# A hybrid SSM and attention layer on one core: the output product's weight sums made in DRAM during the attention, its operand sums made in DRAM and rounded in the middle of products, and the last residual tiles loaded into room of their own

## The chip, the cores and the metric

The kernel runs on one core of a Trainium2 chip. The metric is the device time of one execution in microseconds (us). A run executes the kernel and gives one time; a second record, the profiled execution, gives the span from the first to the last instruction and the trace of every engine and DMA.

The engines go by these names: PE (TensorE, matmuls), ACT (ScalarE), DVE (VectorE), POOL (GpSimd) and SP (SyncE, which only issues DMAs). ACT and POOL issue DMAs too. Each engine works its instructions in program order.

## What is computed

One encoder layer on a sequence of 512 rows of width 2048, all in float32: a state space scan on 4 groups (branch A, y) and an attention of 16 heads (branch B, o), merged by gates. Cut from the reference:

```
    h = rmsnorm(x, norm_w)
    u = h @ w_in
...
    y_fwd = ssd_scan(xs, dtf, a_f, bm, cm)
...
    y = y.reshape(b, s, D_SSM) * jax.nn.silu(z_ssm)
...
    o = bidir_attention(qn, qr, kn, kr, v) * jax.nn.silu(z_attn)

    merged = jax.nn.sigmoid(g_ssm) * (y @ w_proj_ssm) + jax.nn.sigmoid(g_attn) * (o @ w_proj_attn)
    return x + merged @ w_out
...
    return rmsnorm(x, final_norm_w)
```

The change touches `merged @ w_out`, the residual add and the last normalisation. Rows come in four tiles `t` of 128, columns in four blocks `b` of 512.

## The kernel before

**Arithmetic.** A float32 product is made of three matmuls on rounded parts: each operand x is split into a high part (a cast on ACT) and a low part (x minus high, on DVE), and PE does high x high, high x low and low x high (lines 605 to 607). `w_split` splits a weight chunk of 128 x 1024 this way (lines 433 and 434) into `wh` and `wl`, three buffers each. ACT and DVE do this for every chunk in program order, so whatever stands ahead of a chunk's split on ACT or DVE holds PE up once three chunks are used up.

**Stages.** Input projection, state space scan, attention, and then three products of 512 x 2048 x 2048, named by their weights `wps` (y), `wpa` (o) and `wo` (merged, the output product). Each is one level of Strassen: `pair(cp)` computes one half of the output columns by seven products P1 to P7, each with four weight chunks m = 0..3 and 48 matmuls. The order is P1, P5, P6, P2, P3, P7, P4, except for the first pair of `wo` (`early`): P1, P2, P5, P6, P3, P7, P4. The activation operands are x11, x12, x22 and sums S1 to S4. The weight operands are blocks of w and sums: T1 = w00 + w01, T2 = T1 + w11 (`t2`), T3 = w11 + w01, and T4 = T2 + w10 (`t4`). `X` and `Y` are four chunk buffers each; `wraw` has three.

**Where the sums are made before.** For `wps` and `wpa`, T1 and T3 are made in DRAM ahead of time: `t_jobs` yields a list of DMAs on POOL, a copy DRAM to DRAM of 512 KB and, two copies later, an accumulate onto it; `in_background(n)` issues the next n. The 32 of `wps` run in the scan, the 32 of `wpa` in the attention, four per head behind a small POOL multiply (`pace`) that waits for the head's softmax sums. For `wo` they are made in SBUF: `w_more` (line 532) lets POOL issue an accumulating DMA of w01 onto an `X` or `Y` chunk after its plain use.

The activation operands of `wo` are made from the results of `wpa`: `done_pa` turns each block on PE (`turn`), and ACT moves it out. Blocks of x11, x21 and S3 go to DRAM (`m_d`). S4 and x22 stand raw in SBUF (`m_raw`, placed by `m_room`), S2 raw in two `xraw` tiles; POOL's accumulating DMAs add the later blocks there (lines 1474 and 1482). `Merged.split` rounds a whole operand on ACT and DVE (lines 433, 434; 436 for S2, which has its sign turned): S2 after P2, S4 and x22 after P5, S3 after P6, by the table of hooks in `Strassen("wo", ...)`.

**The end.** A finished block of the output gets its residual: for t < 2 or b < 2 by an accumulating DMA of x on POOL (line 1649), else by a DVE add from a `gate` tile that POOL loads late (lines 1625, 1645). ACT squares each block with a running sum (line 1639, `scr`). `final_weights` loads the final gains broadcast (`fw`); `weigh` multiplies the blocks of t >= 2 by them on POOL (line 1636). `finish(t)` computes the row scale r and scales and stores the four blocks of a row tile: t = 0 and 1 one product after P3 of the second pair, t = 2 and 3 from the last product (`last_o`). All stores go out on SP.

Of the kernel before, what the change touches and what calls it, by code (L numbers as in the profile page):

```python
# [18 lines left out]
P = 128  # L19
# [53 lines left out]
def build(tc, a):  # L73
# [48 lines left out]
    m_d = {w: scratch(f"m_{w}", 2048) for w in ("x11", "x21", "S3")}  # L122
# [3 lines left out]
    t_d = {(w, cp, n): scratch(f"{n}_{w}{cp}", 4096) for w in ("wps", "wpa") for cp in range(2) for n in ("T1", "T3")}  # L126
# [273 lines left out]

    def za_gen(i):
        p_ = mm("za")
        yield from gemm_steps(p_, win(T_ZA + i), h_h, h_l)
        g_ = st("za")
        act.activation(g_, p_, AF.Silu)
        put(za_d[i], g_)

# [60 lines left out]
    class Merged:  # L468
# [9 lines left out]
        def load(self, which, src, tiles):  # L478
            self.raws[which] = tiles
            for q, t in enumerate(tiles):  # L480
                tc.keep_in_program_order(pool.dma_start(t, src[:, q * 1024:(q + 1) * 1024]))
# [22 lines left out]
    def t_jobs(w):  # L504

        jobs = []
        for cp in range(2):
            for name, kh, cb in (("T1", 0, 0), ("T3", 1, 1)):
                for m in range(4) if (w, cp, name) in t_d else ():
# [79 lines left out]
    def product(name, op, chunk, extra=None, pre=None):  # L589
# [3 lines left out]
        for m in range(4):  # L593
# [4 lines left out]
            if pre and m == 2:  # L598
# [31 lines left out]
    class Strassen:  # L630
# [65 lines left out]
        def pair(self, cp, headed=False, early=False):  # L696
# [44 lines left out]
            def t3(m, raw):  # L741
                w_more(raw, w, cp, 0, 1, m)
# [3 lines left out]
            p5 = evict((yield from product("P5", self.op("S1"), c5, t2)), "p5", self.kept("C22", cp))  # L746
            self.hook(cp, "P5")
            A = yield from product("P6", self.op("S2"), lambda m: X[m])
# [8 lines left out]
            B = yield from product("P3", self.op("S4"), lambda m: Y[m], None if made3 else t3,  # L757
# [421 lines left out]

    compressed(0, 6, rq_d, V_QN, cq_h, cq_l)  # L1180
# [6 lines left out]
    fill.run(36)  # L1187

# [24 lines left out]
    fill.run(36)  # L1213
    dve.tensor_scalar(ang2, ang, math.pi / 2, None, ALU.add)
# [5 lines left out]
    fill.run(48)  # L1220

# [113 lines left out]
    fill.until(("qk", 0))  # L1335
    fill.run(24)

    heads = {}
    in_background(len(background))
    background.extend(t_jobs("wpa"))  # L1340
    pace = few(1)

    def scores(hd, t):
# [16 lines left out]
        if background and t == 1:  # L1360
            pool.tensor_mul(pace, sm_, sm_)
            in_background(4)
# [90 lines left out]
    def done_pa(t, b, o):  # L1453
# [3 lines left out]
        def turn():  # L1457
# [13 lines left out]
            elif t < 2:  # L1471
                o_ = st("turned")
                act.activation(o_, tp, AF.Copy, scale=-1.0)
                pool.dma_start(m_ops.raw("S4", q, u), o_, accum_op=ALU.add)
                m_ops.into(w, o_, sl.start, SEQ)
            else:
                s1, raw = (m_ops.raw(n, q, u) for n in ("S1", "x22"))
                dve.tensor_sub(s1, s1, tp)
                act.activation(raw, tp, AF.Copy, scale=-1.0)
                m_ops.into("S1", s1, sl.start, SEQ)  # L1480
                for n in ("S2", "S4"):
                    pool.dma_start(m_ops.raw(n, q, u), raw, accum_op=ALU.add)
# [3 lines left out]
    m_ops = Merged()  # L1486

# [3 lines left out]
    def m_room():  # L1491
# [280 lines left out]
```

## Time and profile before

| what | value |
|---|---|
| three runs | 2051.38, 2042.46, 2047.32 us; median 2047.32 |
| the profiled execution | 2045.46 us, its span 2043.7 us |
| mean granted PE clock | 0.987 |
| busy: PE, DVE, ACT, POOL | 95%, 75%, 49%, 18% of the span |
| DMA moved | 393.25 MB, mean 192 GB/s |
| the output product on PE | 1842.93 to about 2028.5 us of the span |

How to read the rows: times are us from the start of the span. A row of an engine's timeline has start, duration, engine, source line, operation, output and inputs by the program's names, shape and count; in square brackets is the idle time of the engine before it and what ended that. A DMA row has the issuing queue, the KB of each and the median us from issue to landing. A row of waits has total, number and longest. Rows of the windows view have the stretch, its length, then busy time (and number of instructions) of PE, PE's weight load, DVE, ACT and POOL, the granted clock, the DMA share and GB/s.

### The profile page before, as it was taken

What the parts mean: (1) busy time and instruction counts of PE and PEld (TensorE: products, weight loads), DVE (VectorE), ACT (ScalarE), POOL (GpSimd) and SP (SyncE); (2) the same over time, 40 slices, a digit from 0 to 9 for tenths busy, and PEclk for the clock granted to TensorE, in tenths of its full rate; (3) what the DMA queues carried; (4) which work ended last, traced back from release to release, by engine and by line L of the source; (5) the groups of instructions that cost most, each with busy time, mean ns of one, the idle gap of its engine ahead of it and who ended that gap; (6) DMA issues with size and microseconds to landing.
All of it is one profiled execution on the core that took longest, in us unless ns stands there. A gap on an engine that the chain in (4) does not pass through costs nothing.

```text
span 2043.7 us, 24735 instructions
## 1 busy us (share of the span) xinstructions
PE 1945.2 (95%) x8978; PEld 1602.9 (78%) x8978; DVE 1532.7 (75%) x2016; ACT 1000.6 (49%) x1392; POOL 363.4 (18%) x405
## 2 busy tenths in 40 slices
PE   6999999999999999999999999999999999998796
PEld 5878888888878778787788788888877788886675
DVE  7976676676759889799795767667677898786675
ACT  6444445444544656546555344444455355444453
POOL 0001001001032252342430101110011110213113
PEclk9999999999999999999999999999999999999998
DMA  5568658647456747687574957873487886978746
GB/s 195 164 181 206 164 126 205 170 124 201 130 174 180 236 145 206 207 242 206 172 200 139 256 159 178 224 191 99 99 254 256 275 301 211 308 220 218 208 84 184
DMA packets 169898, 393.25 MB, mean 192 GB/s; under 512 B 16752, under 2 KB 61936, under 8 KB 169584
## 3 DMA queue, kind: packets, MB, share of 16 engines
q1 hardware_dynamic: 102384, 229.94, 34.4%
q0 software_dynamic: 36448, 119.03, 26.6%
q10 hardware_dynamic: 30944, 42.71, 5.8%
q8 instruction: 70, 1.15, 0.2%
q14 instruction: 52, 0.43, 0.1%
HBM read 334.47 MB, written 100.14 MB: 213 GB/s over the span
## 4 chain that ended last, share of the span: by engine, by line
PE 65%; DVE 13%; DMA 9%; issue 7%; ACT 3%; POOL 1%; SPq 0%; ACTq 0%; DVEq 0%; POOLq 0%
PE P L606 11%; PE P L607 11%; PE P L605 11%; PE za L168 2%; PE xbc L168 2%; PE za L169 2%; PE xbc L169 2%; PE za L170 2%; PE xbc L170 2%; DVE sum L1092 2%; DVE wl L434 2%; DVE wl L164 1%; DMA stack<-qr 1%; DMA wraw<-wps 1%; PE pb L1369 1%
## 5 line engine op out<-in xcount | busy, mean ns | idle before, releaser
L434 DVE TENSOR_TENSOR wl<-X,wh 128x1024 fp32r<-128x1024 f32 x180 | 219.4, 1223 | 100.9 <-ACT wh L433 100.8
L433 ACT CAST wh<-X 128x1024 fp32r<-128x1024 f32 x180 | 188.9, 1053 | 203.2 <-PE P L607 162.1
L164 DVE TENSOR_TENSOR wl<-wraw,wh 128x1024 fp32r<-128x1024 f32 (+2 forms) x148 | 176.4, 1192 | 82.4 <-ACT wh L163 80.2
L163 ACT CAST wh<-wraw 128x1024 fp32r<-128x1024 f32 (+2 forms) x150 | 145.0, 969 | 129.4 <-PE xbc L169 38.6
L434 DVE TENSOR_TENSOR wl<-Y,wh 128x1024 fp32r<-128x1024 f32 x96 | 117.1, 1223 | 79.1 <-ACT wh L433 79.1
L433 ACT CAST wh<-Y 128x1024 fp32r<-128x1024 f32 x96 | 100.9, 1053 | 137.0 <-PE P L607 104.3
L168 PE MATMUL xbc<-h_h,wh 128*128 128x512 f32 x384 | 152.7, 398 | 0.0
L170 PE MATMUL xbc<-h_h,wl 128*128 128x512 f32 x384 | 150.6, 392 | 0.0
L169 PE MATMUL xbc<-h_l,wh 128*128 128x512 f32 x384 | 150.4, 392 | 0.0
L606 PE MATMUL P<-wl,h_h 128*128 128x512 f32 x384 | 149.5, 389 | 0.0
L607 PE MATMUL P<-wh,h_l 128*128 128x512 f32 x384 | 149.4, 389 | 0.0
L605 PE MATMUL P<-wh,h_h 128*128 128x512 f32 x384 | 149.4, 389 | 0.0
L606 PE MATMUL P<-wl,S 128*128 128x512 f32 x288 | 112.5, 391 | 0.8 <-DVE wl L434 0.7
L607 PE MATMUL P<-wh,S 128*128 128x512 f32 x288 | 112.1, 389 | 0.0
L605 PE MATMUL P<-wh,S 128*128 128x512 f32 x288 | 112.1, 389 | 0.0
L168 PE MATMUL za<-h_h,wh 128*128 128x512 f32 x256 | 101.1, 395 | 0.0
L170 PE MATMUL za<-h_h,wl 128*128 128x512 f32 x256 | 99.9, 390 | 0.0
L169 PE MATMUL za<-h_l,wh 128*128 128x512 f32 x256 | 99.6, 389 | 0.0
L433 ACT CAST wh<-wraw 128x1024 fp32r<-128x1024 f32 x56 | 58.9, 1052 | 81.9 <-PE P L607 55.9
L434 DVE TENSOR_TENSOR wl<-wraw,wh 128x1024 fp32r<-128x1024 f32 x56 | 68.4, 1223 | 39.6 <-ACT wh L433 39.6
L1092 DVE TENSOR_TENSOR_SCAN sum<-da,scn 128x512 f32<-128x512 f32 x64 | 86.3, 1361 | 0.0
L1356 ACT ACTIVATE pr<-s,nm 128x512 f32<-128x512 f32 x64 | 44.2, 690 | 84.0 <-DVE nm L1354 83.2
(727 smaller groups left out, 5264.0 us busy)
## 6 DMA issues: line engine op xcount, KB each, us to landing
wraw<-wi SPq DMA_DIRECT2D x102, 512.0 KB, 4.0
T_wps<-wps POOLq DMA_DIRECT2D x32, 512.0 KB, 6.3
da<-da_d SPq DMA_DIRECT2D x64, 256.0 KB, 4.4
T_wpa<-wpa POOLq DMA_DIRECT2D x32, 512.0 KB, 9.2
wraw<-wps SPq DMA_DIRECT2D x24, 512.0 KB, 5.8
xbc_d<-xbc ACTq DMA_DIRECT2D x24, 256.0 KB, 3.3
wraw<-wun SPq DMA_DIRECT2D x16, 384.0 KB, 3.1
wraw<-wo SPq DMA_DIRECT2D x12, 512.0 KB, 4.1
```

The source lines that it names most:

```text
L163: act.copy(h, raw)
L164: (dve if ahead[0] else pool).tensor_sub(l, raw, h.bitcast(F32))
L168: pe.matmul(out, wh, xh, start=start, stop=False)
L169: pe.matmul(out, wh, xl, start=False, stop=False)
L170: pe.matmul(out, wl, xh, start=False, stop=stop)
L433: i = act.copy(hi_, raw)
L434: dve.tensor_sub(lo_, raw, hi_.bitcast(F32))
L605: pe.matmul(bs[i], xh, wh, start=(j == 0), stop=False)
L606: pe.matmul(bs[i], xh, wl, start=False, stop=False)
L607: pe.matmul(bs[i], xl, wh, start=False, stop=(j == 7))
L1092: dve.tensor_tensor_scan(sums[dd], flat(da), mask, 0.0, ALU.add, ALU.mult)
L1356: act.activation(pr, s, AF.Exp, bias=nm, scale=SCALE, accum_out=sm_)
```

## The change

The order of PE's instructions stays the same. The diff, cut to its core:

```
-    m_d = {w: scratch(f"m_{w}", 2048) for w in ("x11", "x21", "S3")}
+    m_d = {w: scratch(f"m_{w}", 2048) for w in ("x11", "x21", "S2", "S3", "S4")}
...
-    t_d = {(w, cp, n): scratch(f"{n}_{w}{cp}", 4096) for w in ("wps", "wpa") for cp in range(2) for n in ("T1", "T3")}
+    t_d = {(w, cp, n): scratch(f"{n}_{w}{cp}", 4096) for w in ("wps", "wpa", "wo") for cp in range(2) for n in ("T1", "T3")}
...
+    paced = [None]
+    pace = few(1)
+
+    def at_pace(t, n):
+        if background:
+            pool.tensor_mul(pace, t[:, 0:1], t[:, 0:1])
+            in_background(n)
...
             def t3(m, raw):
-                w_more(raw, w, cp, 0, 1, m)
+                if not made3:
+                    w_more(raw, w, cp, 0, 1, m)
                 if early:
                     t4_alone(m, raw)
...
+    in_background(len(background))
+    background.extend(t_jobs("wpa"))
+    background.extend(t_jobs("wo"))
     compressed(0, 6, rq_d, V_QN, cq_h, cq_l)
...
+    at_pace(paced[0], 3)
...
-        if background and t == 1:
-            pool.tensor_mul(pace, sm_, sm_)
-            in_background(4)
+        if t == 1:
+            at_pace(sm_, 4)
...
             elif t < 2:
                 o_ = st("turned")
                 act.activation(o_, tp, AF.Copy, scale=-1.0)
-                pool.dma_start(m_ops.raw("S4", q, u), o_, accum_op=ALU.add)
+                pool.dma_start(m_d["S4"][:, sl], o_, accum_op=ALU.add)
                 m_ops.into(w, o_, sl.start, SEQ)
             else:
-                s1, raw = (m_ops.raw(n, q, u) for n in ("S1", "x22"))
+                s1, o_ = m_ops.raw("S1", q, u), st("turned")
                 dve.tensor_sub(s1, s1, tp)
-                act.activation(raw, tp, AF.Copy, scale=-1.0)
+                act.activation(o_, tp, AF.Copy, scale=-1.0)
                 m_ops.into("S1", s1, sl.start, SEQ)
-                for n in ("S2", "S4"):
-                    pool.dma_start(m_ops.raw(n, q, u), raw, accum_op=ALU.add)
+                m_ops.into(w, o_, sl.start, SEQ)
+                pool.dma_start(m_d["S2"][:, sl], o_, accum_op=ALU.add)
+                s4_owed.append((m_d["S4"][:, sl], o_))
+                while u and s4_owed:
+                    d, raw = s4_owed.pop(0)
+                    pool.dma_start(d, raw, accum_op=ALU.add)
...
+    def m_copies():
+        for n in ("S4", "S2"):
+            tc.keep_in_program_order(pool.dma_start(m_d[n], m_d["S3"]))
...
     def weigh(t, b):
-        if t >= 2:
+        if t >= 2 or b < 3:
             pool.tensor_mul(res[t, b], res[t, b], room["fw"][:, b])
...
             if b == 3:
-                finish(t)
+                due.append(t)
...
-        room["fw"] = xa.tile([P, 4, SEQ], F32, tag="opa", bufs=2, name="fw")
+        t_ = room["fw"] = xa.tile([P, 8, SEQ], F32, tag="opa", bufs=2, name="fw")
...
+        for t in (2, 3):
+            for b in (2, 3):
+                act.dma_start(x_late(t, b), x_of(t, b))
...
-            if b == 2 or t < 2:
+            if b == 2 and t >= 2 or b == 3 and t < 2:
                 dve.scalar_tensor_tensor(o, o, r, room["fw"][:, b], ALU.mult, ALU.mult)
-            elif b == 1:
+            elif b == 1 or b == 2:
                 dve.tensor_scalar_mul(o, o, r)
...
-            nc.sync.dma_start(a["out"][t * P:(t + 1) * P, b * SEQ:(b + 1) * SEQ], o)
+            (nc.sync if b % 2 == 0 else act).dma_start(a["out"][t * P:(t + 1) * P, b * SEQ:(b + 1) * SEQ], o)
...
         def before():
-            pre()
             for i in range(2):
-                dve.tensor_sub(u[i], fetched[2 + i, 2], u[i])
+                dve.tensor_sub(u[i], x_late(2 + i, 2), u[i])
+            for t in due:
+                finish(t)
...
     wo = Strassen("wo", m_ops, -1, done_o, fetch_o, {
-        (0, "P2"): [m_split("S2")],
-        (0, "P5"): [m_split("S4", "x22"), m_place("S3"), m_load("S3", "S3", w_raw)],
-        (0, "P6"): [m_split("S3")], (1, "P2"): [final_weights]}, kept_o, last_o)
+        (0, "P2"): [m_load("S2", "S2", w_raw)], (0, "P5 mid"): [m_split("S2")],
+        (0, "P5"): [m_load("S4", "S4", w_raw)], (0, "P6 mid"): [m_split("S4")],
+        (1, "P2"): [final_weights]}, kept_o, last_o)
```

The line `at_pace(paced[0], 3)` stands at four places ahead of head 0: behind the loads of the rope key, twice among the rope tables, and just before the heads; `paced[0]` is the last `za` tile that ACT wrote. With `wo` in `t_d`, `pair` takes T1 and T3 of the output product by plain loads on SP (`t_load`). "P5 mid" and "P6 mid" are hooks in the last chunk (m = 3) of these products. The table of `wpa` changes with it: the copies of S3 into S4 and S2 stand after P6 of its second pair, S3 is loaded after P3 and split after P7, and the raw x21 for S1 is loaded on SP.

POOL's queue around the start of the output product. `m_raw` and `xraw` are the raw operands in SBUF, `p` the blocks of P2's result, `m_S_197` before is S3 in DRAM; before:

```order
L532 DMA X<-wo 128x1024
L1482 DMA m_raw<-m_raw 128x512
L1482 DMA xraw<-m_raw 128x512
L1482 DMA m_raw<-m_raw 128x512
L1482 DMA xraw<-m_raw 128x512
L1482 DMA m_raw<-m_raw 128x512
L1482 DMA xraw<-m_raw 128x512
L1482 DMA m_raw<-m_raw 128x512
L1649 DMA p_15693<-x 128x512
L1649 DMA p_15696<-x 128x512
L481 DMA xraw<-m_S_197 128x1024 x2
L532 DMA Y<-wo 128x1024 x4
```

The same place now; `m_S_197` is S2 in DRAM here and `m_S_199` is S4:

```order
L1500 DMA m_S_199<-turned 128x512
L1496 DMA m_S_197<-turned 128x512
L1500 DMA m_S_199<-turned 128x512
L1496 DMA m_S_197<-turned 128x512
L1500 DMA m_S_199<-turned 128x512
L1668 DMA p_15752<-x 128x512
L1668 DMA p_15755<-x 128x512
L490 DMA xraw<-m_S_197 128x1024 x2
L490 DMA xraw<-m_S_199 128x1024 x2
L1668 DMA kk<-x 128x512 x2
```

The accumulates of weights onto X and Y are gone, the operand accumulates go to DRAM, and the loads of S2 and S4 stand behind the residual accumulates of P2's blocks.

ACT from the last chunk of P2 to the chunks of P6 (`wh` is a weight chunk's high part, `scr` a square, `ms` P5's result); before:

```order
L433 CAST wh<-wraw 128x1024
L436 ACTIVATE S__15292<-xraw 128x1024
L433 CAST wh<-X 128x1024
L436 ACTIVATE S__15292<-xraw 128x1024
L433 CAST wh<-X 128x1024 x5
L1639 ACTIVATE scr,small<-p_15693 128x512
L568 COPY ms<-P_15703 128x512
L568 COPY ms<-P_15704 128x512
L433 CAST wh<-X 128x1024
```

and now:

```order
L442 CAST wh<-wraw 128x1024
L442 CAST x__15458<-turned 128x512
L442 CAST wh<-X 128x1024 x4
L1658 ACTIVATE scr,small<-p_15752 128x512
L442 CAST wh<-X 128x1024
L1658 ACTIVATE scr,small<-p_15755 128x512
L445 ACTIVATE S__15141<-xraw 128x1024
L442 CAST wh<-X 128x1024
L445 ACTIVATE S__15141<-xraw 128x1024
L577 COPY ms<-P_15762 128x512
L577 COPY ms<-P_15763 128x512
L442 CAST wh<-X 128x1024 x2
```

S2's split (line 436, now 445) moves from ahead of P5's chunks to among P6's first two chunks, behind the squares of P2's blocks.

POOL at the entry of the attention (`yn_S` are operand sums of y, `k` the rope key's halves, `krb` its low part); before:

```order
L1397 DMA yn_S_213<-yn_x_211 512x512
L1394 DMA yn_S_215<-yn_S_213 16x16384
L1185 DMA k_9187<-kr_d 32x512
L1186 DMA k_9188<-kr_d 32x512
```

and now:

```order
L1411 DMA yn_S_219<-yn_x_217 512x512
L406 TENSOR_TENSOR small<-za 128x1
L521 DMA T_wpa_206<-wpa 128x1024 x3
L1408 DMA yn_S_221<-yn_S_219 16x16384
L1199 DMA k_9193<-kr_d 32x512
L1200 DMA k_9194<-kr_d 32x512
```

A pace multiply and three copies stand ahead of the last operand copy and the key's loads.

More of the change, by code (lines that the diff above doesn't have):

```diff
@@ L406, in za_gen @@
         put(za_d[i], g_)
+        paced[0] = g_
     def qkv_gen(i, sq, new):
@@ L587, in turn_bank, with product @@
         return SETS[used[1]][i]("turn")
-    def product(name, op, chunk, extra=None, pre=None):
+    def product(name, op, chunk, extra=None, pre=None, pre_at=2):
         used.append((used[-1] + 1) % 4)
@@ L1335, in build @@
     fill.until(("qk", 0))
+    at_pace(paced[0], 3)
     fill.run(24)
     heads = {}
-    in_background(len(background))
-    background.extend(t_jobs("wpa"))
-    pace = few(1)
     def scores(hd, t):
@@ L1622, in fetch_o @@
     def fetch_o(t, b):
-        if late(t, b):
-            fetched[t, b] = st("gate")
-            pool.dma_start(fetched[t, b], x_of(t, b))
+        pass
     def kept_o(tag, cp, i):
```

46 lines of the change are left out of this document (24 added, 22 removed).

## Prediction

> **What bounds the kernel now.** First the page: busy time by engine.
>
> ```profile
> span 2043.7 us, 24735 instructions
> PE 1945.2 (95%) x8978; PEld 1602.9 (78%) x8978; DVE 1532.7 (75%) x2016; ACT 1000.6 (49%) x1392; POOL 363.4 (18%) x405
> ```
>
> TensorE (PE) sets the time: 98.5 us of the span are without a matmul, and the change removes no matmul. So only idle or slowly clocked TensorE time can be won, and I look for where it lies: the windows view of four stretches (stretch, its length, busy time of PE, PEld, DVE, ACT, POOL, granted clock, DMA share, GB/s).
>
> ```profile
> 1195.00:1360.00 165.00, 162.91 (x860) 137.52 (x858) 111.06 (x222) 72.21 (x144) 26.70 (x44) 1.00 0.74 192
> 1360.00:1520.00 160.00, 153.22 (x773) 126.46 (x772) 109.97 (x218) 73.93 (x142) 8.56 (x11) 1.00 0.51 139
> 1720.00:1843.00 123.00, 123.00 (x572) 102.20 (x571) 101.44 (x115) 58.16 (x66) 27.14 (x45) 1.00 0.79 252
> 1843.00:1960.00 117.00, 97.52 (x395) 76.87 (x393) 69.88 (x74) 50.87 (x68) 24.56 (x29) 0.93 0.82 202
> ```
>
> The third row is the second half of the attention product, whose weight sums already come from DRAM: no idle. The fourth is the first half of the output product: 19.5 us idle at clock 0.93. Then the waits of TensorE from 1843 to 2029 (engine, line, what it waited for; total, times, longest), and its rows in order of time.
>
> ```profile
> PE P L606 <- DVE wl L434: 11.8, 8, 5.9
> PE P L605 <- ACT wh L433: 10.3, 5, 4.8
> ```
> ```profile
> 1785.84 0.39 PE L605 MATMUL P<-wh,S__14156 128*128 128x512 f32 x1
> ...
> 1796.72 0.39 PE L605 MATMUL P<-wh,x__13885 128*128 128x512 f32 x1
> ...
> 1842.14 1.03 PE L1460 MATMUL turn<-cst,p 128*128 128x128 f32 x8
> 1842.93 0.48 PE L605 MATMUL P<-wh,x__14922 128*128 128x512 f32 x1
> ...
> 1874.88 0.79 PE L605 MATMUL P<-wh,S__15096 128*128 128x512 f32 x1 [4.85 <-ACT wh L433]
> ...
> 1918.25 0.79 PE L606 MATMUL P<-wl,S__15797 128*128 128x512 f32 x1 [5.94 <-DVE wl L434]
> 1918.84 0.63 PE L607 MATMUL P<-wh,S__15797 128*128 128x512 f32 x1
> 1919.27 0.63 PE L605 MATMUL P<-wh,S__15797 128*128 128x512 f32 x1
> ...
> 1939.80 0.50 PE L605 MATMUL P<-wh,x__15514 128*128 128x512 f32 x1 [2.46 <-ACT wh L433]
> 1941.06 0.77 PE L606 MATMUL P<-wl,x__15514 128*128 128x512 f32 x1 [0.76 <-DVE wl L434]
> ...
> 2005.45 0.49 PE L605 MATMUL P<-wh,S__15797 128*128 128x512 f32 x1 [1.17 <-ACT wh L433]
> ```
>
> Two undisturbed products start 10.88 us apart (1785.84, 1796.72); eight transposes take 0.79. The output product starts at 1842.93, and its twelfth product ends at 2005.45 - 1.17 = 2004.28. Undisturbed it would end at 1842.93 + 0.79 + 12 x 10.88 = 1974.3. So **30.0 us** are lost: 22.1 us waited in all, less the 1.17 at the thirteenth product, makes 20.9; the other 9.1 are slow matmuls: after the 5.94 us wait they start 0.43 us apart (1918.84, 1919.27) instead of 10.88/48 = 0.227.
>
> What the splits waited for (ACT and DVE feed every weight chunk in program order), in ACT's rows, then DVE's, then the DMA view from 1840 on (issuing queue, count, KB each, median us to landing):
>
> ```profile
> 1872.84 1.06 ACT L436 ACTIVATE S__15292<-xraw 128x1024 fp32r<-128x1024 f32 x1 [6.95 <-DMA xraw<-m_raw]
> 1935.44 0.63 ACT L1639 ACTIVATE scr<-kk 128x512 f32<-128x512 f32 x1 [5.16 <-DMA kk<-x]
> ```
> ```profile
> 1915.23 1.23 DVE L734 TENSOR_TENSOR X<-X,wraw 128x1024 f32<-128x1024 f32 x1 [5.55 <-DMA wraw<-wo]
> ```
> ```profile
> Y<-wo POOLq DMA_DIRECT2D x8, 512.0 KB, 8.2
> m_raw<-m_raw POOLq DMA_DIRECT2D x4, 256.0 KB, 13.5
> xraw<-m_S POOLq DMA_DIRECT2D x2, 512.0 KB, 7.4
> ```
>
> P5's wait is ACT standing on S2, whose SBUF accumulates land after 13.5 us; P7's is DVE standing on a weight chunk queued beside the Y accumulates (8.2); P4's is ACT standing on a residual accumulate.
>
> **The change part by part.**
>
> *Weight sums and operands of the output product.* Sixteen weight accumulates and eight SBUF accumulates leave POOL; as many plain loads of T1 and T3 take their place on SP, in the form that the 1720 row shows without idle. ACT no longer splits S2 ahead of P5's chunks: the order sets it ahead of P6. At most all of the loss goes: **-30**. What is late next, with both ends:
> - P1/P2: DVE and ACT take S3 earlier, x22 directly. 0 to 2, taken 1.
> - P6: S2's loads stand on POOL behind the two residual accumulates of P2, which wait for DVE's P2 sums; a load like it took 7.4 us, and P5 covers 10.88. 0 to 4.9 (P5's wait of today), taken 2, since that leaves 3.5 for the sums and the issue.
> - P3/P7: the extra chunks of T4 still use one buffer chain. 0 to 5.9, taken 1.5, since the Y accumulates beside it are gone.
> - P4: the residual accumulate before it stays as it is. 0 to 3.2 (2.46 + 0.76), taken 2.
> - Slow matmuls: by today's ratio 9.1/20.9 these 6.5 us would draw 2.8; taken 1.5, since they are short (0 to 7).
>
> Sum **+8** (0 to 23). The clock deserves a look: the 0.43 us pitch follows the wait of 5.94 and also P4's pair 2.46 and 0.76. The Trainium skill (TensorE: Matmul & The Clock Gate, "Part 1: The HAM clock gate") says that the array falls to half rate after an idle window of about 3.4 us and returns after as much busy time. The trace agrees for 5.94; 3.2 us in two pieces lies just below. By that rule alone waits of 2 us draw nothing, and the sum would be 1.5 us lower.
>
> *Second half of the attention product.* It gains two 1 MB copies on POOL, S3's loads, and S3's split on ACT (2 x 1.06) and DVE (2 x 1.23). The 1720 row has DVE free for 21.6 us of 123. **0** (0 to 2); with that cover gone the two splits would cost 2.5.
>
> *More background sums.* Of the 32 more DRAM jobs twelve come before head 0 (next part); heads 8 to 12 now have four each, as heads 0 to 7 had. What one such job takes, from the page:
>
> ```profile
> T_wpa<-wpa POOLq DMA_DIRECT2D x32, 512.0 KB, 9.2
> ```
>
> Of the first two rows of the windows the 1195 row is with such jobs (DMA share 0.74), the 1360 row without (0.51), which it will have. TensorE idles 2.1 us of 165 with them against 6.8 of 160 without: the heads' own loads are early enough to bear the company. **0** (-2 to +5, about the difference of the two).
>
> *Entry of the attention.* Three copies stand on POOL ahead of the last operand copy and of the rope key's loads, nine jobs more with their waits ahead of, or just behind, the MEMSET of krb.
>
> ```profile
> 1180.61 0.58 PE L1284 MATMUL vp<-wh,ckv_h 128*128 128x256 f32 x1 [2.76 <-ACT za L405]
> ```
>
> TensorE waits here already: behind the key's loads stand DVE's rope, then ACT, whose eviction of za comes behind the casts of the key. So later keys pass through in full once the wait is there. 0 to 9.2 (one job's landing), taken **+3**, a third, since the issues share the DMA engines rather than wait for each other.
>
> *Tail.* The residual tiles of the last rows are loaded early; POOL's ten multiplies by the final weights stand ahead of the last residual accumulates.
>
> ```profile
> 1999.49 2.53 POOL L1636 TENSOR_TENSOR ms<-ms,fw 128x512 f32<-128x512 f32 x2 [1.88 <-DMA fw<-fnw]
> ...
> 2009.12 1.79 POOL L1649 DMA_DIRECT2D big<-x  x2 [2.66 <-DVE big L664]
> ```
> ```profile
> 2030.90 0.69 DVE L1687 TENSOR_TENSOR big<-gate,big 128x512 f32<-128x512 f32 x1 [1.30 <-DMA gate<-x]
> ```
>
> Ten multiplies at 2.53/2 = 1.27 end at 2012.2, so the accumulates go out 3.1 us later. Against it: the 1.30 us wait goes, DVE's eight products by r and weights for rows 0 and 1 become two such and four by r alone, and the stores use two queues. The cheaper passes set against the delay, the wait is left: **-1** (-3 to +3, the delay alone either way).
>
> *Sum against the profiled execution:* 2043.7 - 30 + 8 + 0 + 0 + 3 - 1 = 2023.7 us of span. That execution took 2045.46, 1.76 beyond its span: 2025.5. The median of the runs, 2047.32, is 1.9 above it: **2027**.
>
> **The rivals.**
>
> *No wait comes back* (0.16): every unknown at its low end but one us: 2043.7 - 30 - 3 + 1 = 2011.7, so 2015. For it speaks the 1720 row, idle-free at 252 GB/s; against it that this stage also has the residuals and the S2 and S4 round trips.
>
> *The DMA engines stay full* (0.13). The bytes of weights in the stage are the same; only who issues them changes. Its row has share 0.82 at 202 GB/s. If landings stay at 8 to 13 us, P6 waits 4.9, P7 5.9, P4 3.2, P2 1: 15.0, with slow matmuls in today's ratio (x 1.44) 21.5 instead of 8: 2040.5. The Trainium skill (DMA: Bandwidth & Descriptors, "Issuing engines are not separate DMA queues") has it so: all queues interleave on the same 16 engines, and spreading brings no bandwidth. Against: share 0.79 carries 252 GB/s in the 1720 row, so the accumulates cost engine time that plain loads do not.
>
> *The entry pays a whole landing* (0.07): +9 instead of +3: 2033.
>
> *The DRAM accumulates follow one another* (0.06; the slower side). S2 and S4 are now summed in DRAM, eight accumulates alternating on one queue from about the time of the first today:
>
> ```profile
> 1846.88 0.85 POOL L1482 DMA_DIRECT2D xraw<-m_raw  x1 [0.51 <-DMA xraw<-m_S]
> ...
> 1859.78 1.91 POOL L1482 DMA_DIRECT2D m_raw<-m_raw  x1
> ```
>
> If each waited for the landing of the one before, L us, S2 would be whole after seven, and loaded 7.4 later; P6 could start at 1842.93 + 0.79 + 3 x 10.88 = 1876.4. With L = 9.2 (the DRAM jobs): 1846.9 + 64.4 + 7.4 - 1876.4 = 42 us of wait in place of the 2: 2067. It decides from L = 7.8 on, where P6 waits 32.6 us and the time passes 2057.6. Against: today's eight go out within 13 us, and S2 is read 13.1 us after the last, so they overlap.
>
> **How the numbers follow.** The forecast has 0.58. A measurement here can tell 0.5%, about 10 us: faster means under 2037, slower over 2057.6. Faster: 0.58 + 0.16 + 0.07 = 0.81; same: 0.13; slower: 0.06. The range 2014 to 2041 leaves out the last rival and half of the full-DMA case, under 2 in 10.
>
> **What would show it.** Right: the 1843 row's successor has 4 to 8 us idle at a clock of 0.97 or more, P5 starts without a wait, landings of T1 and T3 are about 5 us, and the rest of the gain stays to the end. Wrong: ACT standing on S2 or S4 ahead of P6 or P3 for more than 5 us; TensorE idle for over 6 us around head 0; or DVE's last chain starting behind POOL's multiplies by more than 3 us.

## The result and the profile after

The changed kernel is slower by 0.8%. Seven runs have a median of 2060.83 us (2056.41 to 2066.99), seven of the kernel before 2045.88 (2038.86 to 2051.38): the ratio is 1.0082, with a 95% interval of 1.0058 to 1.0105. The forecast was 2027 with a range of 2014 to 2041, so size and sign are wrong. The profiled span is 2056.4 us, 12.7 more than before.

The windows view of the changed kernel, to set beside the rows of before (heads with jobs; later heads, which now have jobs; the last heads; the second half of the attention product from the same matmul to the same; the output product's first 114 us, its rest up to the thirteenth product, and the tail):

```profile
1195.00:1360.00 165.00, 161.21 (x856) 136.53 (x854) 111.70 (x225) 73.30 (x146) 26.39 (x44) 1.00 0.82 214
1360.00:1460.00 100.00, 96.34 (x490) 80.46 (x489) 65.80 (x130) 42.70 (x83) 11.61 (x20) 0.98 0.71 185
1460.00:1530.00 70.00, 63.21 (x289) 50.92 (x288) 45.96 (x90) 32.49 (x60) 14.94 (x21) 0.96 0.82 204
1727.30:1855.50 128.20, 125.09 (x572) 103.22 (x570) 100.57 (x114) 59.86 (x68) 24.96 (x41) 0.99 0.79 261
1855.50:1969.70 114.20, 98.47 (x406) 78.63 (x404) 74.79 (x80) 51.77 (x71) 16.24 (x20) 0.93 0.72 207
1969.70:2011.60 41.90, 41.90 (x183) 34.55 (x183) 35.63 (x34) 20.57 (x21) 6.45 (x5) 0.98 0.33 93
2011.60:2056.40 44.80, 22.21 (x97) 17.75 (x95) 22.38 (x52) 13.66 (x29) 16.16 (x12) 0.81 0.42 137
```

The second half of the attention product took 123 us before, without idle; now it takes 128.2 for the same 572 matmuls. The output product still has 15.7 us of idle in its first stretch, at the old clock of 0.93. The tail, 38.2 us from the start of the thirteenth product before, is 44.8.

Following single matmuls through both traces splits the 12.7 us: 0.1 up to the middle of head 2 (a matmul at 1254.28 before, 1254.34 now); 7.0 us lost from there to the second product of the scan's weights (1529.11 before, 1536.13 now); 5.5 more up to the output product (1842.93, 1855.48); 6.4 **won** in it up to its thirteenth product; 6.5 lost behind that.

The 0.1 hides a wait at the entry of the attention. First a load of weights that SyncE issues there (window 1180 to 1202), before; then the same load now, with the rows of ACT and TensorE that follow from it:

```profile
wraw<-wur SPq DMA_DIRECT2D x1, 384.0 KB, 3.3
```
```profile
wraw<-wur SPq DMA_DIRECT2D x1, 384.0 KB, 10.3
1205.99 0.83 ACT L163 CAST wh<-wraw 128x768 fp32r<-128x768 f32 x1 [4.95 <-DMA wraw<-wur]
1207.36 0.50 PE L1362 MATMUL s<-kh,qh 128*128 128x512 f32 x1 [2.46 <-ACT kh L1319]
```

With background jobs beside it the load lands late (10.3 us after its issue instead of 3.3), ACT stands on it, and the cast of the first key stands behind. Before, TensorE has no wait at this matmul (1207.19).

Where the last heads wait, by ACT's rows and then TensorE's:

```profile
1497.04 1.05 ACT L442 CAST wh<-wraw 128x1024 fp32r<-128x1024 f32 x1 [3.67 <-DMA wraw<-wps]
```
```profile
1502.34 0.41 PE L1383 MATMUL pb<-cst,pr 128*128 128x128 f32 x2 [2.72 <-DVE pr L1373]
...
1519.02 0.41 PE L1383 MATMUL pb<-cst,pr 128*128 128x128 f32 x2 [3.15 <-DVE pr L1373]
```

The first weights of the scan's product come late; ACT stands on one, and softmax and transposes stand behind ACT and DVE. The jobs have run on POOL until just before, in the first row here; the operand sums of the attention, second row, go out 13 us later than before (1471.76 there), because the store of a head's output that they read landed 14.5 us after its issue, against 3.6 before (it landed at 1484.29; the row names a load that landed at 1484.86):

```profile
1471.16 0.81 POOL L522 DMA_DIRECT2D T_wo<-wo  x1 [2.21 <-DMA T_wo<-wo]
1484.90 2.33 POOL L1411 DMA_DIRECT2D o_S<-o_x  x2 [12.93 <-DMA stack<-qr]
```

TensorE's waits from 1855 to 2036, and the two rows that matter (ACT, then DVE):

```profile
PE turn L1474 <- DVE u L1469: 7.5, 2, 6.2
PE P L614 <- ACT wh L442: 6.5, 2, 4.4
PE P L615 <- DVE wl L443: 3.1, 4, 1.4
```
```profile
1869.79 0.60 ACT L1493 ACTIVATE turned<-turn 128x512 f32<-128x512 f32 x1 [8.31 <-DMA m_S<-turned]
```
```profile
1845.83 0.69 DVE L1468 TENSOR_TENSOR p<-p,gate 128x512 f32<-128x512 f32 x1 [6.09 <-DMA gate<-ga_d]
```

S2 no longer stops ACT ahead of P5. In its place ACT stands at the second of the last four turned blocks: it may not write the tile `turned` before the two DRAM accumulates that read the block before it have landed (issued at 1859.07 and 1859.64, landed at 1867.12 and 1869.68). Weight chunks and the blocks of P4 stand behind. The DVE row lies in the attention product's last product: a gate that lands late.

The tail, by POOL's rows:

```profile
2006.89 3.53 POOL L1655 TENSOR_TENSOR p<-p,fw 128x512 f32<-128x512 f32 x2 [3.01 <-DMA fw<-fnw]
2010.38 3.51 POOL L1655 TENSOR_TENSOR kk<-kk,fw 128x512 f32<-128x512 f32 x2
2013.86 2.55 POOL L1655 TENSOR_TENSOR ms<-ms,fw 128x512 f32<-128x512 f32 x2
2016.36 3.52 POOL L1655 TENSOR_TENSOR p<-p,fw 128x512 f32<-128x512 f32 x2
2019.84 3.52 POOL L1655 TENSOR_TENSOR big<-big,fw 128x512 f32<-128x512 f32 x2
2023.30 1.78 POOL L1668 DMA_DIRECT2D big<-x  x2
```

Ten multiplies take 16.4 us, and the last residual accumulates go out at 2023.3, 11.7 us after the thirteenth product's start; before it was 3.7.

### The profile page after: what moved, and what is told of

It is laid out like the page before. It is cut to its first block, busy times and chain, and to the rows that moved or that the text cites. A ratio compares the mean times of both kernels' runs of the same rounds, so it can differ in the third digit from the quotient of the medians.

```text
span 2056.4 us, 24806 instructions
## 1 busy us (share of the span) xinstructions
PE 1947.4 (95%) x8978; PEld 1603.9 (78%) x8978; DVE 1532.1 (75%) x2016; ACT 1003.5 (49%) x1396; POOL 383.9 (19%) x432
## 4 chain that ended last, share of the span: by engine, by line
PE 57%; DVE 16%; DMA 12%; issue 9%; ACT 4%; POOL 2%; ACTq 0%; SPq 0%; DVEq 0%; POOLq 0%
PE P L615 9%; PE P L616 9%; PE P L614 9%; DMA wraw<-wps 3%; DVE sum L1103 2%; DVE wl L443 2%; PE za L168 2%; PE za L169 2%; PE za L170 2%; DVE wl L164 2%; PE xbc L168 2%; PE xbc L169 2%; PE xbc L170 2%; PE pb L1383 1%; PE qp L168 1%
```

## The experiments

The kernels were timed in four groups, and the kernel before was run anew with each: its median was 2045.88 us beside the changed kernel, 2044.36 beside the next four rows of the table, 2043.53 beside those from "six per head" to "copies elsewhere", and 2042.60 beside the last two. So kernels of different groups are compared by their ratios, not by their medians. The table has the medians, the ratios to the runs of before in the same group, and from each trace: "heads", the delay gained against before between the middle of head 2 and the scan's second product (the entry lies ahead of it); "half", the second half of the attention product from its P1 to the output product's start; "output", from there to the thirteenth product's start; "P1", the first product of the output product; "tail", from the thirteenth product's start to the end (us).

| kernel | median | ratio (95%) | heads | half | output | P1 | tail |
|---|---|---|---|---|---|---|---|
| before | 2045.88 | 1 | 0 | 79.9 | 162.5 | 13.1 | 38.2 |
| changed | 2060.83 | 1.0082 (1.0058, 1.0105) | 7.0 | 85.1 | 156.1 | 21.2 | 44.8 |
| own room for turned blocks | 2057.20 | 1.0059 (1.0037, 1.0081) | 8.4 | 90.1 | 149.5 | 13.2 | 44.7 |
| few multiplies | 2054.99 | 1.0056 (1.0034, 1.0077) | 4.2 | 84.8 | 157.8 | 21.4 | 37.5 |
| no output weight sums | 2060.38 | 1.0087 (1.0064, 1.0109) | 0.7 | 88.2 | 157.5 | 21.9 | 44.8 |
| weight sums alone | 2042.75 | 0.9991 (0.9977, 1.0004) | 7.0 | 79.8 | 149.2 | 13.6 | 40.1 |
| the same, six per head | 2037.87 | 0.9973 (0.9958, 0.9987) | -1.2 | 79.8 | 149.6 | 13.3 | 39.9 |
| operand sums alone | 2046.18 | 1.0029 (1.0013, 1.0044) | -1.1 | 83.4 | 161.1 | 22.1 | 38.5 |
| six per head and tail | 2030.42 | 0.9941 (0.9928, 0.9954) | 2.5 | 79.8 | 147.0 | 14.4 | 37.4 |
| copies elsewhere | 2069.95 | 1.0128 (1.0111, 1.0145) | 6.6 | 84.2 | 156.2 | 21.8 | 45.3 |
| three remedies | 2042.68 | 1.0008 (0.9990, 1.0026) | -1.3 | 86.6 | 150.4 | 13.1 | 37.4 |
| and late S3 | 2042.98 | 1.0000 (0.9983, 1.0016) | -1.3 | 81.0 | 158.2 | 13.7 | 37.4 |

**Own room for turned blocks.** The edit, in the changed kernel (a place of S2's size is taken one hook earlier, and S2 takes the same place at its split):

```
-                s1, o_ = m_ops.raw("S1", q, u), st("turned")
+                s1, o_ = m_ops.raw("S1", q, u), m_ops.home[:, sl]
...
-        (1, "P6"): [m_place("S2"), m_copies], (1, "P2"): [m_place("x12")],
+        (1, "P6"): [m_place("S1"), m_copies], (1, "P2"): [m_place("x12")],
...
-        (0, "P2"): [m_load("S2", "S2", w_raw)], (0, "P5 mid"): [m_split("S2")],
+        (0, "P2"): [m_load("S2", "S2", w_raw)], (0, "P5 mid"): [m_place("S2"), m_split("S2")],
```

> The changed kernel, with one thing different: the last four turned blocks (x22) go to raw room of their own, the place that S2's operand takes later, instead of a tile of the three that gates and turned blocks share. Nothing is left out. Theory (a wait for room took the place of the one removed): ACT's 8.3 us wait at the second of these blocks for the accumulates of the first goes, and with it TensorE's waits of 6.23 and 1.22 us before the second product and 2 to 3 us of slow matmuls. From the start of the output product to the start of its thirteenth product 156.1 us become 146, and the time falls by about 10 us to 2051. Rival (the DMA engines are full, landings of 7 to 10 us): the wait moves to the next load or operand, the stretch stays over 153 us, and the time changes by less than 4 us.

ACT's rows at the four blocks:

```profile
1865.53 0.60 ACT L1493 ACTIVATE home<-turn 128x512 f32<-128x512 f32 x1 [2.28 <-DVE xraw L1492]
...
1867.26 0.60 ACT L1493 ACTIVATE home<-turn 128x512 f32<-128x512 f32 x1
...
1877.28 0.60 ACT L1493 ACTIVATE home<-turn 128x512 f32<-128x512 f32 x1 [0.93 <-DVE xraw L1492]
...
1878.81 0.60 ACT L1493 ACTIVATE home<-turn 128x512 f32<-128x512 f32 x1
```

No block waits for a DMA, and P1 takes 13.2 us instead of 21.2. The wait for room is shown, at 8 us. The stretch came to 149.5, though, not 146, and the ratio fell only from 1.0082 to 1.0059, with intervals that overlap: in this run the second half of the attention product took 5 us more than in the changed kernel. That half is the unsteadiest stretch of all runs with DRAM operand sums (81.0 to 90.1), and two of its products alone vary: P2 (10.9 to 16.6 us, 11.0 before), whose weight chunks land late, and P4 (11.8 to 17.6, 11.8 before), whose gate does.

**Few multiplies.**

```
-        if t >= 2 or b < 3:
+        if t >= 2:
...
-            if b == 2 and t >= 2 or b == 3 and t < 2:
+            if b == 2 or t < 2:
...
-            elif b == 1 or b == 2:
+            elif b == 1:
```

> The changed kernel with POOL's multiplies by the final weights as they were: only for rows of t >= 2, four ahead of the last residual accumulates instead of ten, and the eight products by r and weights for rows 0 and 1 on DVE. Nothing is left out. Theory (POOL became the bound of the tail): the last residual accumulates go out at the latest 1 us after the sums they wait for instead of 11, DVE's last chain starts some 8 us earlier, and from the start of the thirteenth product to the end 44.8 us become about 39; the time falls by 5 to 6 us. Rival (the tail waits for the loads of final weights and residual tiles, or for the deferred scaling, whoever multiplies): 43 us or more, and less than 2 us in the time.

POOL's rows:

```profile
2006.32 3.52 POOL L1655 TENSOR_TENSOR ms<-ms,fw 128x512 f32<-128x512 f32 x2 [2.92 <-DMA fw<-fnw]
2009.80 3.54 POOL L1655 TENSOR_TENSOR p<-p,fw 128x512 f32<-128x512 f32 x2
2013.29 1.78 POOL L1668 DMA_DIRECT2D big<-x  x2
```

The accumulates go out 2.2 us after the thirteenth product's start (2011.1) instead of 11.7, and the tail takes 37.5 us: 7.3 less. The ratio falls from 1.0082 to 1.0056, some 5 us, with intervals that overlap; it is the tail that shows the theory to hold, here and in the three later kernels with four multiplies (37.4 each).

**No output weight sums.** Two edits: `"wo"` leaves the table `t_d`, and its jobs leave the background list.

```
-    t_d = {(w, cp, n): scratch(f"{n}_{w}{cp}", 4096) for w in ("wps", "wpa", "wo") for cp in range(2) for n in ("T1", "T3")}
+    t_d = {(w, cp, n): scratch(f"{n}_{w}{cp}", 4096) for w in ("wps", "wpa") for cp in range(2) for n in ("T1", "T3")}
...
-    background.extend(t_jobs("wo"))
```

> The changed kernel without the output product's weight sums in DRAM: T1 and T3 of the output product are again made by accumulates on POOL in the product, the background jobs are the 32 of the attention product alone and end with head 4. Nothing of the result is left out. Theory (the jobs in heads 8 to 12 delay the last heads): the 7.3 us that the first matmul of the scan's product loses go, to under 2. The output product then pays for its accumulates again, 10 us or more, so that the time is not better than that of the changed kernel by more than 3 us. Rival (the last heads are late for another reason, by chance or by the jobs at the entry): the scan's product starts as late as with the jobs, within 2 us.

The heads lose 0.7 us, so the jobs are what costs 7. The time did not gain by it: the accumulates onto Y now stand among POOL's ten multiplies, and P7 of the second pair waits 7.70 us:

```profile
2011.05 11.02 DVE L443 TENSOR_TENSOR wl<-Y,wh 128x1024 fp32r<-128x1024 f32 x1 [1.93 <-ACT wh L442]
2018.23 2.74 POOL L1654 TENSOR_TENSOR big<-big,fw 128x512 f32<-128x512 f32 x2
2022.12 0.79 PE L615 MATMUL P<-wl,S__15295 128*128 128x512 f32 x1 [7.70 <-DVE wl L443]
```

What it waits for is not an accumulate: that chunk had landed at 2009.87, and ACT had made its high part. DVE's subtraction of it took 11.02 us instead of 1.22 and ended 1.1 us after the last of the ten multiplies. The accumulates of the next two chunks were late as well (2017.13 and 2020.06).

**Weight sums alone.** The kernel before with the hunks of the diff on `t_d`, `at_pace`, the start of the jobs and `t3`, and no other:

```
+    t_d = {(w, cp, n): scratch(f"{n}_{w}{cp}", 4096) for w in ("wps", "wpa", "wo") for cp in range(2) for n in ("T1", "T3")}
...
+    background.extend(t_jobs("wpa"))
+    background.extend(t_jobs("wo"))
...
+            at_pace(sm_, 4)
```

> The kernel before with one part of the change alone: the output product's weight sums are made in DRAM during the attention, with the same pace and the same start of the jobs as in the change. Operand sums in SBUF, residual tiles and tail stay as before. Nothing is left out. Theory: the scan's product starts about 7 us late as in the changed kernel, the waits for the accumulates onto Y (5.94 us) go, S2's wait (4.85) stays, the tail stays at 38.3 us; in sum within 5 us of the kernel before. Rival (the jobs cost nothing in the heads, the +7 comes from elsewhere): 8 to 12 us faster than before.

The heads lose 7.0 us; the output product is 13.3 us shorter than before, the attention product's second half is as before. In sum there is no difference that can be told. (Up to the middle of head 2 this profile is 7.5 us behind before's, 4 of them from the scan, which the change doesn't touch, the rest from the entry; so it is read by stretches.) The theory holds but for one point: S2's wait ahead of P5 did not stay at 4.85 us. With its sums still in SBUF it fell to 1.95:

```profile
1883.92 0.49 PE L614 MATMUL P<-wh,S__15141 128*128 128x512 f32 x1 [1.95 <-ACT wh L442]
```

With the operand sums left out the weight sums win twice what the whole change won there.

**Six per head.** One number in it:

```
-            at_pace(sm_, 4)
+            at_pace(sm_, 6)
```

> The kernel before with the output product's weight sums in DRAM alone, as in the run of that part, but with six background jobs per head instead of four, so that they end with head 8 and not with head 12. Nothing is left out. Theory (the jobs meet the operand sums of the attention and the first weights of the scan's product in the last heads): the 7 us lost between the start of the heads and the scan's product shrink to under 2, and the time falls by about 5 us, to 2038, faster than the kernel before by 0.3%. Rival (the jobs cost what they move, wherever they stand): the 7 us stay, spread over heads 0 to 8, and the time is that of four per head, 2043 within 2.

The last heads in the windows view, 1360 to 1460 and 1460 to 1530, before:

```profile
1360.00:1460.00 100.00, 96.34 (x504) 80.77 (x503) 66.43 (x132) 43.65 (x86) 0.00 (x0) 1.00 0.38 106
1460.00:1530.00 70.00, 66.88 (x319) 53.94 (x318) 49.90 (x98) 35.02 (x67) 11.57 (x16) 1.00 0.75 206
```

and with six per head:

```profile
1360.00:1460.00 100.00, 96.34 (x509) 81.09 (x508) 66.13 (x132) 43.93 (x86) 5.43 (x8) 1.00 0.54 148
1460.00:1530.00 70.00, 66.78 (x320) 54.17 (x320) 49.76 (x98) 34.76 (x65) 11.65 (x16) 1.00 0.75 205
```

The last row has 3.2 us of idle (3.1 before) where the changed kernel has 6.8 at a clock of 0.96. The heads lose nothing (-1.2), though the same jobs now stand closer: up to 1360 the DMA share is 0.90 (0.74 before), and the last job goes out at 1384.4. The time is 0.27% under before (0.13% to 0.42%), against 0.09% with four per head, whose interval overlaps. What the jobs cost depends on where they stand, not on what they move.

**Operand sums alone.** The kernel before with the hunks on S2 and S4 (`m_d`, the hooks, `turn`, `m_copies`, `m_load`), and no other:

```
+    m_d = {w: scratch(f"m_{w}", 2048) for w in ("x11", "x21", "S2", "S3", "S4")}
...
+                pool.dma_start(m_d["S2"][:, sl], o_, accum_op=ALU.add)
...
+        (0, "P2"): [m_load("S2", "S2", w_raw)], (0, "P5 mid"): [m_split("S2")],
+        (0, "P5"): [m_load("S4", "S4", w_raw)], (0, "P6 mid"): [m_split("S4")],
```

> The kernel before with the other large part of the change alone: S2 and S4 of the output product summed in DRAM and rounded in the middle of products, with the copies, the turned blocks in the three shared tiles and the loads as in the change. Weight sums of the output product by accumulates as before, tail as before. Nothing is left out. Theory (this part costs by itself): the second half of the attention product and its end lose 4 to 11 us to late weights and late gates, ACT waits 8 us at the second x22 block, S2's wait of 4.85 us ahead of P5 goes; the time is 5 to 12 us above before. Rival (the part is sound, and its losses come from the loads of the weight sums beside it): within 3 us of before, or faster.

The stretches are as the theory says: 3.5 us lost in the attention product's second half, P1 at 22.1 us, S2's wait gone. The ratio is 0.29% above before (0.13% to 0.44%), 5.9 us, though the medians are only 2.7 apart: the low end of the 5 to 12 expected, since the output product as a whole is still 1.4 us shorter than before. So this part costs by itself. Its ACT waits 10.95 us for the accumulates:

```profile
1862.45 0.60 ACT L1480 ACTIVATE turned<-turn 128x512 f32<-128x512 f32 x1 [10.95 <-DMA m_S<-turned]
```

**Six per head and tail.** The run of six per head, with the change's hunks on `x_late`, `due`, `final_weights`, `finish` and `last_o`, and the edit of few multiplies:

```
+                act.dma_start(x_late(t, b), x_of(t, b))
...
+            (nc.sync if b % 2 == 0 else act).dma_start(a["out"][t * P:(t + 1) * P, b * SEQ:(b + 1) * SEQ], o)
...
+                dve.tensor_sub(u[i], x_late(2 + i, 2), u[i])
+            for t in due:
+                finish(t)
```

> The run with six jobs per head, with the change's tail added except for POOL's six extra multiplies: residual tiles of the last rows loaded early into room of their own, scaling of rows 0 and 1 deferred, stores on two queues. Nothing is left out. Theory (the tail's other parts are good for 1 to 3 us once POOL is not in the way): from the start of the thirteenth product to the end 36 to 38 us, and the time 1 to 3 us under that of six jobs per head, the best of all, about 2036. Rival (the residual loads meet the last accumulates, and the deferred scaling stands before the last sums): 39 us or more, and no gain.

The tail takes 37.4 us against 39.9, and the time falls by 7.5 to 2030.42, 0.59% under before (0.46% to 0.72%): more than the 1 to 3 us expected. Some 2.5 us of it lie in the tail and as much in the output product; the rest is not placed. It is the fastest of all.

**Copies elsewhere.**

```
-            tc.keep_in_program_order(pool.dma_start(m_d[n], m_d["S3"]))
+            tc.keep_in_program_order(pool.dma_start(m_d[n], h_d["S3"]))
...
-        (0, "P6"): [C(o_ops, "x22")],
+        (0, "P6"): [C(o_ops, "x22"), m_copies],
...
-        (1, "P6"): [m_place("S2"), m_copies], (1, "P2"): [m_place("x12")],
+        (1, "P6"): [m_place("S2")], (1, "P2"): [m_place("x12")],
```

> The changed kernel with the two 1 MB copies that start S2 and S4 in DRAM issued in the first half of the attention product, from another tensor of the same size (h's S3): S2 and S4 start from wrong values, their traffic is moved out of the second half, all else is the same. Theory (the copies crowd out the weights of P2 and the gates of P4): the second half of the attention product is without waits again, and the output product starts 4 to 5 us earlier, 275 to 276 us after the start of the scan's first P5 product instead of 280 to 286. Rival (S3's loads into the weight buffers and the weights of the output product that then come all at once are to blame): only P2's 1 us goes, the late gate with its 4 us stays.

The rival holds: P2's 1 us went, the late gate stayed, and the half took 84.2. The copies do cost, but where they stand: in the first half ACT now waited for a chunk of weights whose load took 14.8 us beside them (8.7 for the same load in the changed kernel). The stretch from the scan's second product to the second half grew by 4.2 us, and the time rose by 9; the rest is not placed.

```profile
1713.48 1.04 ACT L442 CAST wh<-X 128x1024 fp32r<-128x1024 f32 x1 [7.35 <-DMA X<-T_wpa]
```

**Three remedies.** Own room, six per head and few multiplies together in the changed kernel:

```
+                s1, o_ = m_ops.raw("S1", q, u), m_ops.home[:, sl]
...
+            at_pace(sm_, 6)
...
+        if t >= 2:
```

> The changed kernel with the three remedies together: room of their own for the last four turned blocks, six background jobs per head, POOL's multiplies for rows of t >= 2 only. Nothing is left out. Against the run of six jobs per head with the tail, the difference is then that S2 and S4 are summed in DRAM. Theory (the three losses are separate, and the operand sums in DRAM still cost in the second half of the attention product): 2060.8 less about 8, 5 and 6, so 2040 to 2043; the heads lose under 2 us, the first product of the output product takes 13 us, the tail from the thirteenth product's start 37 to 38; the second half of the attention product still loses 5 to 10 us, so the time stays about 10 us above the run without DRAM operand sums (2030). Rival (with the room cured the operand sums in DRAM pay): within 3 us of 2030 or under it.

The three add up: by the ratios 15 us under the changed kernel, level with before, and 14 above the run without DRAM operand sums. The second half of the attention product is 6.8 us longer than there, and the output product 3.4.

**Late S3.**

```
-        (1, "P3"): [m_place("S3"), m_load("S3", "S3", w_raw)],
-        (1, "P7"): [m_split("S3"), m_place("x22"), m_load("S1", "x21", y_tile, nc.sync)],
-        (1, "P4"): [m_place("S4")]})
+        (1, "P3"): [m_place("S3")],
+        (1, "P7"): [m_load("S3", "S3", w_raw), m_place("x22"), m_load("S1", "x21", y_tile, nc.sync)],
+        (1, "P4"): [m_split("S3"), m_place("S4")]})
```

> As the run with three remedies, but S3's loads into two of the three weight buffers stand one product later, behind the gates that the last blocks of the attention product wait for, and its split follows one product later too. Nothing is left out. Theory (S3's loads push the gates' issue and landing back): DVE's wait of about 6 us for the gate in the last product of the attention product falls under 2 us and TensorE's 2 us with its slow matmuls behind it, 4 us in all; the time falls by 3 to 5 us. Rival (the gates are late because all queues share full DMA engines there, whoever comes first): the wait only moves to S3's split or to the first weights of the output product, and the time is within 2 us.

The gate in the last product of the attention product, first with three remedies, then with late S3:

```profile
1839.92 0.69 DVE L1468 TENSOR_TENSOR p<-p,gate 128x512 f32<-128x512 f32 x1 [7.82 <-DMA gate<-ga_d]
```
```profile
1841.65 0.69 DVE L1468 TENSOR_TENSOR p<-p,gate 128x512 f32<-128x512 f32 x1 [2.72 <-DMA gate<-ga_d]
```

and ACT with late S3, at the weights of the output product's P2:

```profile
1872.45 1.04 ACT L442 CAST wh<-wraw 128x1024 fp32r<-128x1024 f32 x1 [9.31 <-DMA wraw<-wo]
```

The gate comes in time and the half shrinks by 5.6 us, but the output product grows by 7.8, and the time is the same. The wait has moved, as the rival said: S3's loads use two of three weight buffers, so the weights of the output product, which the kernel before fetched early, come all at once, either before or after the gates: three chunks that before went out from 1799.59 to 1804.19, some 40 us ahead of the output product, go out with late S3 from 1863.22 to 1866.09, when P1 is under way.

## Why the prediction was wrong, step by step

The span was to be 2023.7 us and was 2056.4. By stretches, the output product was to win 22 and won 6.4; the products ahead of it were to lose nothing and lost 5.5; the heads were to lose nothing and lost 7.0; the tail was to win 1 and lost 6.5; the 3 of the entry do not show at head 2.

- **The loss to be won, -30.** Its causes were right: S2's wait ahead of P5 and the Y accumulates' wait in P7 are gone in the changed kernel. With the weight sums alone the stretch fell by 13.3 us, and S2's wait fell to 1.95 by itself; with the room cured, DRAM operand sums gave 149.5 and 150.4 (158.2 with late S3), SBUF ones 147.0 to 149.6. So no run shows a gain from moving S2 and S4, and no run came below 147.0, which is still 15.6 over the undisturbed 131.4. (A small slip: the 22.1 us include 0.77 at 2006.71, behind the thirteenth product's start; 20.2 were waited and 9.8 were slow matmuls.)
- **P1/P2, "0 to 2, taken 1".** This is the step that failed in the output product: 8 us. It looked at how much work ACT and DVE get, not at the tile that the work writes. The order showed `turned` where `m_raw` had been, and `turned` has three buffers shared with the gates; two gates held two of them, so the second block waited for the accumulates of the first. That is a wait put in the place of the one removed, and it came near the rival "the accumulates follow one another": not through the queue, but through the room that they read from.
- **Second half of the attention product, "0 (0 to 2)".** Measured 5.2. The step counted the splits on ACT and DVE and not the copies' and loads' share of the DMA engines, nor that S3's loads take the weight buffers that were used to fetch ahead. The row with 252 GB/s and no idle was read as a proof of room; its first 34 us, from 1763 to 1797, had a DMA share of 0.86 to 1.04.
- **More background sums, "0 (-2 to +5)".** Measured 7.0. The 1360 row's mean share of 0.51 hid what it averages: 0.38 up to 1460 and 0.75 behind it, where the last jobs met the operand sums and the scan's first weights. Six per head, all out by 1384.4, cost nothing at a share of 0.90.
- **Entry, "+3".** Of about the size foreseen, but at another place, and that so little of it is seen at head 2 is chance. At `vp`, where the step looked, TensorE waited 2.75 us (2.76 before). Behind it a weight load took 10.3 us instead of 3.3, and TensorE waited 2.46 and 0.61 us at head 0's first scores, where before it did not wait. From the first matmul of `vp` (1180.61 before, 1179.36 now) to the second group of scores (1209.68, 1210.89) the changed kernel took 2.5 us more, the nine other kernels with these jobs 3.1 to 5.0 more, and operand sums alone, without them, 1.2 less. But this trace came in 1.25 us ahead, and before's own trace lost 1.1 at 1251. The net size is open: counted from the first matmul of `t` (1167.06 before) to head 2, the ten lie between 0.7 less and 3.6 more than before, 1.6 on the mean, and operand sums alone at 3.1 less.
- **Tail, "-1 (-3 to +3)".** Measured +6.5. The accumulates were to go out 6.8 us after the thirteenth product's start (2012.2 against 2005.45) and went out at 11.7. The ten multiplies had been priced at 1.27 us, from a pair that ran while DVE was idle, and took 1.64 on the mean: 3.7 of the 4.9 us. The rest is that the final weights landed 1.2 us later against that start. With four multiplies the tail took 37.5.
- **P6 and P4, "taken 2" each.** P6 started without a long wait; P4 waited 4.42 before its first matmul, behind ACT, which stood 7.12 us on a residual accumulate, and with its slow matmuls lost 8.3. The first two products of the second pair lost 5.4 more, mostly for the same reason; the sum had no term for them.
- **The rivals.** None named this sum. "The DMA engines stay full" was the nearest: landings of weight sums were 5.9 to 7.2 us, not 5. The Trainium skill (DMA: Bandwidth & Descriptors, "Issuing engines are not separate DMA queues") says that queues share the same engines. The entry agrees: beside jobs that POOL issued, SyncE's loads landed after 10.3 us instead of 3.3. Late S3 does not test it, since the weights there were also issued late. The time passed 2057.6, as the last rival had it, but by another way. Of the three signs of being wrong only the third came, in the tail.

What stays open: why P2 and P4 of the second half vary so much between profiles of kernels with DRAM operand sums, what the entry costs net, and where the last 2 to 3 us of the fastest kernel come from.

## What to carry to other kernels

A change that moves a sum or a load off a waiting engine moves it onto something else: for each new tile ask which buffers it shares and what must land before the buffer is free again, and for each engine that gets work ask what is queued behind it. A stage without idle is not a stage with room, and a mean DMA share over a long window does not say whether the last tenth of it is full. Test a compound change by its parts: here one part was good for 0.3% once its pace was set, one cost 0.3% (its waits being traded for others), and a third cost 7 us of the tail for six short multiplies on an engine that was not free.

## What the runs showed of the hardware

A multiply on POOL of 128x512 took 1.27 us where DVE had nothing to do (2.55 for two at 2013.86) and 1.76 beside DVE's splits; one of those splits took 1.82 us beside it instead of 1.22 to 1.23:

```profile
2004.72 1.23 DVE L443 TENSOR_TENSOR wl<-Y,wh 128x1024 fp32r<-128x1024 f32 x1
2007.44 1.82 DVE L443 TENSOR_TENSOR wl<-Y,wh 128x1024 fp32r<-128x1024 f32 x1 [1.50 <-ACT wh L442]
```

The Trainium skill (GPSIMD Engine Reference, "1. Specifications") says that POOL shares its interfaces to SBUF with DVE and contends with DVE instructions that read two inputs there; these rows agree, and price it at about 0.5 us on either side. It can cost far more: without the output weight sums a split of 1.22 us took 11.02 us beside a row of multiplies, and TensorE waited 7.70 for it. Not every pair fits: the last one, at 2019.84, was slow though DVE was idle for the last 2.4 us of its 3.52.

The granted clock fell after the same short waits in one trace and not in the other. In head 12 TensorE waited 1.23 and 0.6 us in both; matmuls behind them started 0.23 us apart before (1458.75, 1458.98) and 0.43 apart in the changed kernel:

```profile
1456.90 0.50 PE L1362 MATMUL s<-kh,qh 128*128 128x512 f32 x1 [1.23 <-ACT kh L1319]
1458.01 0.50 PE L1363 MATMUL s<-kl,qh 128*128 128x512 f32 x1 [0.60 <-DVE kl L1320]
...
1459.30 0.63 PE L169 MATMUL qp<-cq_l,wh 128*128 128x512 f32 x1
1459.73 0.63 PE L170 MATMUL qp<-cq_h,wl 128*128 128x512 f32 x1
```

From 1455 to 1465 the mean granted clock was 1.00 before and 0.83 in the changed kernel. So two waits of 1.8 us together were followed by a slow stretch of 3.4 us, which cost 1.6, or by none, and single profiles differ by such amounts without any cause in the code that was found.
